# First weights from the standing pool, the residual in six parts, conditioning sums over both matrices, stores from ScalarE: edits to a seven-product MLP

## The chip, the cores and the metric

The kernel runs on one core of one Trainium2 chip. The core has a matrix engine (TensorE, PE in the profile) that multiplies operands in on-chip memory (SBUF) and accumulates into eight PSUM banks, and VectorE (DVE), ScalarE (ACT), GpSimd (POOL) and SyncE (SP), each with an instruction queue of its own that runs in order. Transfers between HBM and SBUF are started by an instruction on one of those queues and carried out by 16 DMA engines that all queues share. The metric is the device time of one execution in microseconds; less is better.

## What is computed

One step of a diffusion backbone with two layers on T = 1152 tokens (128 of context, 1024 latent), width 1024, all in fp32. Layer 0 mixes tokens with a recurrent block, layer 1 with latent attention. Behind each mixer stands a squared-ReLU MLP of hidden width 4096, and each sub-layer has an RMS norm, with shift, scale and gate from a linear map of the conditioning vector. The part that matters here, cut from the reference:

```python
def adaln_params(cond, w_ada, b_ada):
    mod = jax.nn.silu(cond) @ w_ada + b_ada
    return jnp.split(mod, 6, axis=-1)

def sq_relu_mlp(h, w1, w2):
    a = jax.nn.relu(h @ w1)
    return (a * a) @ w2
...
for l in range(DEPTH):
    sh1, sc1, g1, sh2, sc2, g2 = adaln_params(...)
    h = modulate(rms_norm(x, norm_mix[l]), sh1, sc1)
    out = mixer(h)
    x = x + g1[:, None, :] * out
    h = modulate(rms_norm(x, norm_mlp[l]), sh2, sc2)
    x = x + g2[:, None, :] * sq_relu_mlp(h, mlp_w1[l], mlp_w2[l])
y = rms_norm(x, final_norm)
```

Context and latent tokens have different conditioning vectors, so each row of `w_ada` is multiplied with two vectors.

## The kernel before

**Layout.** Activations are kept transposed (features on the 128 partitions, 8 blocks of 128 features), in three chunks of 384 tokens. Each fp32 matrix is split into a high and a low part. A product is then three matmuls (`mm3`, L146, L149, L150: high by high, high by low, low by high). The split is a cast on ScalarE (L164) and a subtraction (L165) on VectorE or GpSimd. A weight matrix of 128x1024 (512 KB, one row of `wts`) is loaded into a buffer `raw` (two of them in the standing pool `wp`), split into `whi` and `wlo`, and then `raw` is free.

**One MLP.** `mlp` runs once for each layer ("first" and "second MLP" below). Chunks 0 and 1 go through Winograd's form of Strassen's algorithm, seven block products in place of eight; chunk 2 is computed plainly beside them. The stages in program order:

1. *Fillers* (`filler`, L431): `filler(0, 8)`, eight plain 128-row blocks of the first matrix for chunk 2, 24 matmuls each, while the norms of chunks 0 and 1 are finished and `sums` (L390) makes the sums and differences of chunk 0 and 1 out of X. The norm itself is a generator (`norm_mod`, L294) that the filler steps move on: it yields a number of planned microseconds, `tick` (L359) counts them down.
2. *Up*: the pool of X is released and `upx` opened in its room. Sixteen steps `p`, each with weight sums on VectorE (L446) and seven products. Hidden results, after ReLU and square, are stored to HBM (`hid_d`, nine slots for each of eight groups, two row blocks of 192 KB to a slot) by `put` (L414), which issues on SP.
3. *Change-over*: `upx` is released, X gets new tiles in that room, and its three chunks (1.5 MB each, saved earlier to `xs_d`) are brought back by three DMAs. `load` (L547) brings `hid` tiles of 384 KB and splits them. `filler(8, 8)` does the other eight plain blocks.
4. *Down*: sixteen steps `d`, each with two rows of the second matrix and 22 sub-steps (`step`) of six matmuls; the last two steps leave chunk 2 out and have 14. A row of the second matrix gives two `whi`/`wlo` pairs, the plain one and the one of its differences, which GpSimd makes with four subtractions (L582). Results are added to X from PSUM as they come (`residual`, L332).
5. *End*: `after(0)` and `after(1)`, the next norm of chunks 0 and 1, are queued as generators behind `down2`, eight plain products for chunk 2. In the second MLP the norm is the last one, and its results are stored to the output.

The pairs `whi`/`wlo` take turns over slots as `wcycle` says: "wp" (three in the standing pool), "x" (one), "u" (one in `upx`), and in the down stage "c": a slot in the room of tiles with the tag "G", which also hold an operand of chunk 2 for the fillers.

**Conditioning.** The 56 jobs of `ada` (L175) each load 512 KB of `w_ada` into a `raw` buffer of `wp` and take two dot products on VectorE (L170, one for each conditioning vector). Eight are issued in layer 0's output projection, 40 in the up stage of the first MLP (two or three to a step `p`), and eight in its second set of fillers (`ada_rate`, one for each weight). None are left for the second MLP.

**What sets the order.** The program is not put on the queues in the order in which it is written. A planner simulates it with a time of its own for each instruction, and on each engine takes the ready instruction that stands first in the program. `keep_in_program_order` pins an instruction behind the one traced before it on its engine. A tile waits until the earlier user of its room has been read for the last time. All DMAs that the change touches are issued on SP.

Of the kernel before, what the change touches and what calls it, by code (L numbers as in the profile page):

```python
# [65 lines left out]
class Emit:  # L66
    def __init__(self, nc, tc, ins, outs):
        self.nc, self.tc, self.I, self.O = nc, tc, ins, outs
        self.piece_i = 0
        self.opened = []  # L70
        self.pending = []
        self.wpx = None
        self.pin = False
        self.cap = 1 << 30
        self.upx = None
        self.wcycle, self.wi = ["wp"], 0
        self.ready = []
        self.used, self.oldest = set(), 0
        self.ada_i = 0
        self.ada_jobs = []  # L80
        self.ada_quota = 0.0
        self.ada_rate = 0.0
# [31 lines left out]
    def wslot(self):  # L114

        kind = self.wcycle[self.wi % len(self.wcycle)]
        self.wi += 1
        if kind == "c":
            t = self.cbig(F32R, "wc", "G").rearrange("p a b -> p (a b)")
            return t[:, :1024], t[:, 1024:2048]  # L120
        pool, n = {"wp": (self.wp, 3), "x": (self.wpx, 1), "u": (self.upx, 1)}[kind]
        return tuple(pool.tile([128, 1024], F32R, tag=t, name=t, bufs=n) for t in ("whi", "wlo"))
# [51 lines left out]

    def ada(self, n):  # L175
        for l, j, k in self.ada_jobs[:n]:
            w = self.wp.tile([128, 1024], F32, tag="raw", name="raw", bufs=2)
            n0 = (j * 8 + k) * 128
            self.nc.sync.dma_start(w, self.I["ada_wt"][l, n0:n0 + 128])
            self.ada_dot(w, l, j, k, 0, 1)  # L180
            if k == 7:
                self.mod_finish(l, j)
        del self.ada_jobs[:n]
# [109 lines left out]

    def norm_mod(self, c, x, st, l, js, hi, lo, keep=False):  # L294
        nc = self.nc
        yield 4.0
        y = self.rstd(st, D)
        yield 5.0
        self.modulate(c, x, self.spread(y), l, js, hi, lo, keep=keep)
# [23 lines left out]
    def cbig(self, dt, name, tag="C"):  # L323
        return self.cpool.tile([128, 8, CH], dt, tag=tag, name=name, bufs=6 if tag == "C" else 3)

# [81 lines left out]
    def mlp(self, p0, base, l, H, after_acc, after):  # L407
# [5 lines left out]

        def put(m, slot, t):  # L414
            nc.sync.dma_start(hid_d[m // 4][:, slot, m % 2], t)

# [7 lines left out]
        def drain2(m, c, ps):  # L424
            t = self.cell(tag="acc")
            relu2(t, ps)
            put(m, 5, t)

        rhs = lambda k, c: (H[c][0][:, k], H[c][1][:, k])

        def filler(i0, n):  # L431
            for i in range(i0, i0 + n, 4):
                self.group([(plain[i + j], p0 + i + j, range(8)) for j in range(4)], rhs, drain2, chunks=[2])
# [15 lines left out]
        def prep(p, part):  # L449
            if p == 16:  # L450
                if part:
                    self.cap = p0 + 8 + part
                    self.prefetch(self.cap)
                return
            m = 4 * (p // 2) + p % 2
            if part == 0:
                r = [self.raw(up_row(i), self.upx, 4) for i in (m, m + 2)]
                W[p] = {"r": r, "R0": self.wsplit(r[0], leng)}
                return
            w = W[p]  # L460
            r0, r1 = w["r"]
            a, b = slice(0, 512), slice(512, 1024)
            if part == 1:
                w["R1"] = self.wsplit(r1[:, b], leng, 512)
                add(r0[:, a], r1[:, a], r0[:, a], ALU.subtract)
                add(r1[:, a], r1[:, b], r1[:, a], ALU.subtract)
                add(r1[:, b], r1[:, b], r0[:, a], ALU.subtract)
                add(r0[:, b], r0[:, b], r1[:, b], ALU.subtract)
            else:
                w["TY"] = self.wsplit(r1, nc.vector)  # L470
                w["TX"] = self.wsplit(r0, nc.vector)
# [5 lines left out]
        for p in range(16):  # L477
# [46 lines left out]
            def tail(m=m, A=A, w=w, h11=h11, h12=h12, h22=h22):  # L524
# [3 lines left out]
                add(s, h21, h22)  # L528
                put(m, 4, s)
                add(h21, h11, h21, ALU.subtract)  # L530
                put(m, 6, h21)
                add(d, s, h11, ALU.subtract)
                put(m, 3, d)
                e = st()
                add(e, h12, d, ALU.subtract)
                put(m, 7, e)

            self.ada(3 if p % 2 else 2)
        tail()
# [6 lines left out]

        def load(upto):  # L547
            while used[0] < min(upto, 72):
# [5 lines left out]
                hi, lo = t[:, o:o + 2], t[:, o + 2:o + 4]  # L554
                nc.sync.dma_start(lo.bitcast(F32), hid_d[i // 9][:, i % 9])
                self.split(hi, lo, lo.bitcast(F32))
                D[i] = (hi, lo)
                used[0] += 1

        load(4)  # L560
        for c in range(NCH):
            x = self.xp.tile([128, 8, CH], F32, tag="X", name="X")
            nc.sync.dma_start(x, self.xs_d[l][c])
            self.X.append(x)
        load(12)
        self.ada_rate = 1.0
        filler(8, 8)
        self.ada_rate = 0.0
        self.ada(len(self.ada_jobs))

        self.wcycle, self.wi = ["c", "wp", "wp", "wp", "x", "c", "c"], 0
        V = []
# [19 lines left out]
        prep_down(7)  # L592
        sts_done = []
        for d in range(16):
# [59 lines left out]
        self.wcycle, self.wi = ["wp", "wp", "wp", "x"], 0  # L654
        self.cap = 1 << 30
        self.later(0, after(0))
        self.later(1, after(1))

# [17 lines left out]
    def run(self, stop=99):  # L676
        nc, tc, I, O = self.nc, self.tc, self.I, self.O
        with (
# [21 lines left out]
            cp = self.alloc(name="cpool", bufs=1)  # L700
            self.cpool = cp
            self.ada_jobs = [(l, j, k) for l, j in ADA_ORDER for k in range(8)]
            self.first_half(stop)
# [252 lines left out]
    def rg_out(self, H, stop):  # L956
        nc, I, O = self.nc, self.I, self.O
        hs = self.hs
        nc.sync.dma_start(O["fin"], self.fin)
        self.release(*reversed(self.opened[1:]))  # L960
        self.wpx = self.alloc(name="wpx", bufs=1, side="right", reuse_waits="tile")
# [24 lines left out]
        def after(c):  # L986
            hi, lo = self.hpair2(c)
            nc.sync.dma_start(self.xmid[c], self.X[c])
            self.H3.append((hi, lo))
            yield from self.norm_mod(c, self.X[c], sts[c], 1, 0, hi, lo)  # L990

# [7 lines left out]
    def out_proj(self, pi, Z, l, j):  # L999
# [11 lines left out]
        def after(c):  # L1011
            hi, lo = H2[c] = self.hpair2((2, 0, 1).index(c))
            self.nc.sync.dma_start(self.xs_d[l][c], self.X[c])
            yield from self.norm_mod(c, self.X[c], sts[c], l, j + 1, hi, lo, keep=True)
            if c == 1:
# [25 lines left out]
    def mla(self):  # L1041
# [128 lines left out]
        self.need(None)  # L1170
        self.release(tab, self.cpool)
        self.attention(pi, ckv, kpe)
# [205 lines left out]
    def second_half(self):  # L1378
        nc, O = self.nc, self.O
        self.cpool = self.alloc(name="cpool2", bufs=1, reuse_waits="tile")  # L1380
        self.xp = self.alloc(name="xp2", bufs=3, side="right", reuse_waits="tile")
        Z, self.X = [], []
# [153 lines left out]
```

## Time and profile before

| what | us |
|---|---|
| runs of the kernel | 2876.41, 2880.87, 2880.27 |
| their median | 2880.27 |
| the profiled execution | 2878.42 |
| its span in the profile | 2876.7 |
| first MLP, from the first up product to the norm at its end | about 550 to 1350 |
| second MLP, to the end of the kernel | about 2120 to 2877 |

The page lists the busy time of each engine and, in forty slices of the span, its share. Below the page stand answers of the trace: groups of instructions by source line, the order of single instructions with what each waited for in brackets, and busy time in stretches of the span. In such a row, `ps<-hhi,whi` names what is written and what is read; `L146` is line 146 of the kernel; `[25.93 <-ACT whi L164]` says that the engine stood 25.93 us before this instruction, and that the ScalarE instruction of line 164, which wrote `whi`, released it. PEld is the loading of weights into TensorE. The granted clock is the share of full speed at which the chip ran TensorE.

The memory traffic is 126 GB/s over the span (268.83 MB read, 94.54 MB written).

### The profile page before, as it was taken

The page shows a single profiled execution, that of the slowest core. Times are in us where ns is not written, and L with a number is a line of the kernel's source. Part 1 is how long each engine was busy: PE and PEld are TensorE (multiplying, and loading weights), DVE is VectorE, ACT ScalarE, POOL GpSimd, SP SyncE. Part 2 cuts the span into 40 slices and gives each one's busy share as a digit, 9 for nine tenths or more (in the row PEclk, how much of TensorE's full clock was granted, in tenths as well). Part 3 has the DMA queues.
Part 4 walks back from the last instruction along what each step waited for, and adds up shares of the span by engine and source line. Part 5 has one row for each costly group of instructions (what it writes and reads, how often), then busy time and mean ns, then how long its engine had stood idle before and what let it go on. Part 6 is the DMA issues. An engine that isn't in the chain of part 4 may idle for free.

```text
span 2876.7 us, 41002 instructions
## 1 busy us (share of the span) xinstructions
PE 2655.0 (92%) x15355; PEld 2566.9 (89%) x15355; DVE 1920.1 (67%) x3445; ACT 1389.8 (48%) x2446; POOL 866.5 (30%) x560
## 2 busy tenths in 40 slices
PE   5999999699996899998997999998989999899997
PEld 2878899699995899997997999998989999899996
DVE  6788876999555577777364767762665555277777
ACT  3577834444453233234424878871455555233332
POOL 1000023121212777874242000001200001677773
PEclk9999999899998899999998999999999999999998
DMA  6122243577437334334135111116334445433342
GB/s 251 45 88 81 81 163 133 171 229 220 144 130 265 120 105 137 103 125 139 46 110 170 61 47 53 47 51 210 113 125 147 138 141 189 149 127 115 123 132 101
DMA packets 144855, 368.68 MB, mean 128 GB/s; under 512 B 15376, under 2 KB 77648, under 8 KB 141456
## 3 DMA queue, kind: packets, MB, share of 16 engines
q1 hardware_dynamic: 143888, 362.91, 37.9%
q0 software_dynamic: 768, 3.15, 0.4%
q8 instruction: 121, 1.98, 0.3%
q14 instruction: 78, 0.64, 0.1%
HBM read 268.83 MB, written 94.54 MB: 126 GB/s over the span
## 4 chain that ended last, share of the span: by engine, by line
PE 53%; DVE 5%; DMA 3%; POOL 3%; ACT 2%; issue 2%; SPq 0%; DVEq 0%; POOLq 0%; ACTq 0%
PE ps L146 14%; PE ps L149 13%; PE ps L150 13%; PE ps L1290 2%; DMA raw<-wts 1%; PE ps L1234 1%; PE ps L1237 1%; PE ps L1238 1%; PE ps L1236 1%; PE ps L1235 1%; PE ps L1316 1%; PE ps L1315 1%; POOL wlo L165 1%; PE ps L1314 1%; DMA hid<-hid 1%
## 5 line engine op out<-in xcount | busy, mean ns | idle before, releaser
L165 POOL TENSOR_TENSOR wlo<-raw,whi 128x1024 fp32r<-128x1024 f32 (+1 forms) x177 | 427.1, 2419 | 1643.6 <-ACT whi L164 1028.6
L146 PE MATMUL ps<-hhi,whi 128*128 128x384 f32 x1576 | 539.0, 345 | 76.8 <-ACT whi L164 63.6
L332 DVE SCALAR_TENSOR_TENSOR X<-ps,mod,X 128x384 f32<-128x384 f32 (+2 forms) x768 | 384.2, 536 | 304.7 <-PE ps L150 270.7
L149 PE MATMUL ps<-hlo,whi 128*128 128x384 f32 x1576 | 540.4, 343 | 13.0 <-DVE hlo L319 12.8
L164 ACT CAST whi<-raw 128x1024 fp32r<-128x1024 f32 (+1 forms) x293 | 290.9, 1001 | 539.8 <-PE ps L149 286.7
L150 PE MATMUL ps<-hhi,wlo 128*128 128x384 f32 x1576 | 535.7, 342 | 12.4 <-POOL wlo L165 12.1
L146 PEld LDWEIGHTS ps<-hhi,whi 128*128 128x128 f32 x1576 | 303.3, 193 | 89.1 <-ACT whi L164 67.4
L150 PEld LDWEIGHTS ps<-hhi,wlo 128*128 128x128 f32 x1576 | 303.2, 193 | 17.6 <-POOL wlo L165 16.1
L149 PEld LDWEIGHTS ps<-hlo,whi 128*128 128x128 f32 x1576 | 304.2, 193 | 15.7 <-DVE hlo L319 15.7
L146 PE MATMUL ps<-hid,whi 128*128 128x384 f32 x824 | 278.5, 340 | 8.6 <-ACT whi L164 4.7
L149 PE MATMUL ps<-hid,whi 128*128 128x384 f32 x824 | 278.1, 338 | 0.0
L150 PE MATMUL ps<-hid,wlo 128*128 128x384 f32 x824 | 272.7, 336 | 0.0
L582 POOL TENSOR_TENSOR raw<-raw 128x256 f32<-128x256 f32 x256 | 232.3, 917 | 13.8
L165 DVE TENSOR_TENSOR hid<-hid 128x768 fp32r<-128x768 f32 x144 | 203.8, 1425 | 46.0 <-ACT hid L164 45.8
L165 DVE TENSOR_TENSOR wlo<-raw,whi 128x1024 fp32r<-128x1024 f32 x116 | 134.2, 1167 | 137.6 <-ACT whi L164 137.0
L146 PE MATMUL ps<-hid,wc 128*128 128x384 f32 x584 | 195.6, 338 | 8.1 <-ACT wc L164 6.2
L149 PE MATMUL ps<-hid,wc 128*128 128x384 f32 x584 | 196.7, 337 | 0.0
L150 PE MATMUL ps<-hid,wc 128*128 128x384 f32 x584 | 193.5, 337 | 0.8 <-POOL wc L165 0.8
L164 ACT CAST hid<-hid 128x768 fp32r<-128x768 f32 x144 | 119.7, 836 | 135.7 <-DMA hid<-hid 109.4
L146 PEld LDWEIGHTS ps<-hid,whi 128*128 128x128 f32 x824 | 155.9, 189 | 12.8 <-ACT whi L164 6.6
L165 POOL TENSOR_TENSOR wc<-raw,wc 128x1024 fp32r<-128x1024 f32 x56 | 138.7, 2488 | 77.9 <-ACT wc L164 77.9
L1239 DVE TENSOR_REDUCE mx<-ps 128x1 f32<-128x384 f32 (+1 forms) x200 | 108.6, 543 | 79.7 <-PE ps L1238 78.1
(221 smaller groups left out, 6130.1 us busy)
## 6 DMA issues: line engine op xcount, KB each, us to landing
raw<-wts SPq DMA_DIRECT2D x221, 512.0 KB, 3.7
hid<-hid SPq DMA_DIRECT2D x144, 384.0 KB, 4.5
hid<-st SPq DMA_DIRECT2D x256, 192.0 KB, 1.9
raw<-ada_wt SPq DMA_DIRECT2D x56, 512.0 KB, 3.9
adaw<-ada_n SPq DMA_DIRECT2D x24, 512.0 KB, 4.4
xs<-X SPq DMA_DIRECT2D x6, 1536.0 KB, 5.4
X<-xs SPq DMA_DIRECT2D x6, 1536.0 KB, 10.1
o_d<-o SPq DMA_DIRECT2D x64, 128.0 KB, 1.7
```

Of the source, the lines that this page charges most:

```text
L146: mm = nc.tensor.matmul(ps, lhsT=w[0], rhs=h[0], start=first, stop=False, **kw)
L149: nc.tensor.matmul(ps, lhsT=w[0], rhs=h[1], start=False, stop=False, **kw)
L150: nc.tensor.matmul(ps, lhsT=w[1], rhs=h[0], start=False, stop=last, **kw)
L164: nc.scalar.copy(out=hi, in_=src)
L165: (lo_eng or nc.vector).tensor_tensor(out=lo, in0=src, in1=hi.bitcast(F32), op=ALU.subtract)
L332: self.nc.vector.scalar_tensor_tensor(out=self.X[c][:, m, a:b], in0=ps[:, a:b], scalar=self.mod[:, l, j, cond, m:m + 1], in1=self.X[c][:, ...
L582: sub = lambda out, x, y: nc.gpsimd.tensor_tensor(out=out, in0=x, in1=y, op=ALU.subtract)
L1234: nc.tensor.matmul(ps, lhsT=qh, rhs=kh[:, a:b], start=True, stop=False)
L1235: nc.tensor.matmul(ps, lhsT=qh, rhs=kl[:, a:b], start=False, stop=False)
L1236: nc.tensor.matmul(ps, lhsT=ql, rhs=kh[:, a:b], start=False, stop=False)
L1239: nc.vector.tensor_reduce(out=mx[:, j:j + 1], in_=ps, axis=AX.X, op=ALU.max)
L1290: nc.tensor.transpose(ps[:, j * 128:(j + 1) * 128], p[:, (t * 3 + j) * 128:(t * 3 + j + 1) * 128], self.ident)
```

## The change

1. The first pair of raw weights of the up stage (`p` = 0) is loaded into the two `raw` buffers of `wp` and no longer into `upx`.
2. X is brought back in six halves of 768 KB. Each is issued behind the drain of one filler of the second set (`bring`, called by `drain2`) and pinned there, and with it the next `hid` loads.
3. No conditioning jobs go with the fillers. The up stage takes 24 (one or two to a step), and the other 24 go to the down stage: each use of a slot "g" brings one. These slots are a new pool `gx` (four pairs and a tile `ada` for the conditioning rows), in the room of the former "G" tiles, which are now a pool of their own, `gpool`, released after the last filler. The order of slots in the down stage is four "g", three "wp", one "x".
4. `put` issues on ScalarE's queue, but for the four stores of `tail`, which stay on SP.
5. The store of X (to `xs_d`, and to `xmid` after the first MLP) is issued after the statistics of the norm, not before, and the second planned interval of the norm is 6.0 and not 5.0 us.
6. The norm of chunk 1 at the end of an MLP starts 10.0 planned microseconds later (`behind`).

```diff
@@ wslot
-        if kind == "c":
-            t = self.cbig(F32R, "wc", "G").rearrange("p a b -> p (a b)")
-            return t[:, :1024], t[:, 1024:2048]
-        pool, n = {"wp": (self.wp, 3), "x": (self.wpx, 1), "u": (self.upx, 1)}[kind]
+        if kind == "g":
+            self.ada(1, self.gx)
+        pool, n = {"wp": (self.wp, 3), "x": (self.wpx, 1), "u": (self.upx, 1), "g": (self.gx, 4)}[kind]
@@ ada
-    def ada(self, n):
+    def ada(self, n, room=None):
         for l, j, k in self.ada_jobs[:n]:
-            w = self.wp.tile([128, 1024], F32, tag="raw", name="raw", bufs=2)
+            w = (room or self.wp).tile([128, 1024], F32, tag="ada" if room else "raw", name="raw", bufs=1 if room else 2)
@@ norm_mod
         y = self.rstd(st, D)
-        yield 5.0
+        if store:
+            store()
+        yield 6.0
@@ mlp
-        def put(m, slot, t):
-            nc.sync.dma_start(hid_d[m // 4][:, slot, m % 2], t)
+        def put(m, slot, t, eng=nc.scalar):
+            eng.dma_start(hid_d[m // 4][:, slot, m % 2], t)
...
             put(m, 5, t)
+            if bring2:
+                bring2[0](plain.index(m) - 8)
...
-                r = [self.raw(up_row(i), self.upx, 4) for i in (m, m + 2)]
+                r = [self.raw(up_row(i), *((self.upx, 4) if p else ())) for i in (m, m + 2)]
...
-            self.ada(3 if p % 2 else 2)
+            self.ada(1 + p % 2)
...
-                nc.sync.dma_start(lo.bitcast(F32), hid_d[i // 9][:, i % 9])
+                ld = nc.sync.dma_start(lo.bitcast(F32), hid_d[i // 9][:, i % 9])
+                if pin:
+                    self.tc.keep_in_program_order(ld)
...
-        load(4)
         for c in range(NCH):
-            x = self.xp.tile([128, 8, CH], F32, tag="X", name="X")
-            nc.sync.dma_start(x, self.xs_d[l][c])
-            self.X.append(x)
+            self.X.append(self.xp.tile([128, 8, CH], F32, tag="X", name="X"))
+        xh = [(c, i) for c in range(NCH) for i in (0, 4)]
+
+        def bring(i):
+            if 2 <= i:
+                c, k = xh[i - 2]
+                self.tc.keep_in_program_order(
+                    nc.sync.dma_start(self.X[c][:, k:k + 4], self.xs_d[l][c, :, k:k + 4])
+                )
+            load((2, 4, 5, 6, 7, 8, 9, 9)[i], True)
+
+        filler(8, 8, bring)
         load(12)
-        self.ada_rate = 1.0
-        filler(8, 8)
-        self.ada_rate = 0.0
-        self.ada(len(self.ada_jobs))
-        self.wcycle, self.wi = ["c", "wp", "wp", "wp", "x", "c", "c"], 0
+        self.release(self.gpool)
+        self.gx = self.alloc(name="gx", bufs=1, reuse_waits="tile")
+        self.wcycle, self.wi = ["g", "g", "g", "g", "wp", "wp", "wp", "x"], 0
...
+        self.release(self.gx)
+        self.gpool = self.alloc(name="gpool3", bufs=1, reuse_waits="tile")
+        def behind(us, gen):
+            yield us
+            yield from gen
         self.later(0, after(0))
-        self.later(1, after(1))
+        self.later(1, behind(10.0, after(1)))
@@ after, in rg_out and in out_proj
-            nc.sync.dma_start(self.xmid[c], self.X[c])
...
+            ... store=lambda: nc.sync.dma_start(self.xmid[c], self.X[c])
```

More of the change, by code (lines that the diff above doesn't have):

```diff
@@ L74, in __init__ @@
         self.cap = 1 << 30
-        self.upx = None
+        self.upx = self.gx = None
         self.wcycle, self.wi = ["wp"], 0
@@ L292, in spread, with norm_mod @@
         return r
-    def norm_mod(self, c, x, st, l, js, hi, lo, keep=False):
+    def norm_mod(self, c, x, st, l, js, hi, lo, keep=False, store=None):
         nc = self.nc
@@ L323, in cbig @@
     def cbig(self, dt, name, tag="C"):
-        return self.cpool.tile([128, 8, CH], dt, tag=tag, name=name, bufs=6 if tag == "C" else 3)
+        pool, n = (self.cpool, 6) if tag == "C" else (self.gpool, 3)
+        return pool.tile([128, 8, CH], dt, tag=tag, name=name, bufs=n)
     def hpair2(self, i):
@@ L427, in drain2, with filler @@
             put(m, 5, t)
+            if bring2:
+                bring2[0](plain.index(m) - 8)
         rhs = lambda k, c: (H[c][0][:, k], H[c][1][:, k])
-        def filler(i0, n):
+        bring2 = []
+        def filler(i0, n, f=None):
+            if f:
+                bring2.append(f)
             for i in range(i0, i0 + n, 4):
@@ L528, in tail @@
                 add(s, h21, h22)
-                put(m, 4, s)
+                put(m, 4, s, nc.sync)
                 add(h21, h11, h21, ALU.subtract)
-                put(m, 6, h21)
+                put(m, 6, h21, nc.sync)
                 add(d, s, h11, ALU.subtract)
-                put(m, 3, d)
+                put(m, 3, d, nc.sync)
                 e = st()
                 add(e, h12, d, ALU.subtract)
-                put(m, 7, e)
-            self.ada(3 if p % 2 else 2)
+                put(m, 7, e, nc.sync)
+            self.ada(1 + p % 2)
         tail()
@@ L545, in mlp, with load @@
         used = [0]
-        def load(upto):
+        def load(upto, pin=False):
             while used[0] < min(upto, 72):
@@ L592, in mlp @@
         prep_down(7)
-        sts_done = []
         for d in range(16):
@@ L701, in run @@
             self.cpool = cp
+            self.gpool = self.alloc(name="gpool", bufs=1)
             self.ada_jobs = [(l, j, k) for l, j in ADA_ORDER for k in range(8)]
@@ L959, in rg_out @@
         nc.sync.dma_start(O["fin"], self.fin)
-        self.release(*reversed(self.opened[1:]))
+        self.release(*reversed(self.opened[2:]))
         self.wpx = self.alloc(name="wpx", bufs=1, side="right", reuse_waits="tile")
@@ L987, in after @@
             hi, lo = self.hpair2(c)
-            nc.sync.dma_start(self.xmid[c], self.X[c])
             self.H3.append((hi, lo))
-            yield from self.norm_mod(c, self.X[c], sts[c], 1, 0, hi, lo)
+            yield from self.norm_mod(
+                c, self.X[c], sts[c], 1, 0, hi, lo, store=lambda: nc.sync.dma_start(self.xmid[c], self.X[c])
+            )
         self.pi = self.mlp(pi, pi, 0, H2, lambda c, m: self.sq_acc(sts[c], self.X[c][:, m], m), after)
@@ L1012, in after @@
             hi, lo = H2[c] = self.hpair2((2, 0, 1).index(c))
-            self.nc.sync.dma_start(self.xs_d[l][c], self.X[c])
-            yield from self.norm_mod(c, self.X[c], sts[c], l, j + 1, hi, lo, keep=True)
+            yield from self.norm_mod(
+                c, self.X[c], sts[c], l, j + 1, hi, lo, keep=True,
+                store=lambda: self.nc.sync.dma_start(self.xs_d[l][c], self.X[c]),
+            )
             if c == 1:
@@ L1170, in mla @@
         self.need(None)
-        self.release(tab, self.cpool)
+        self.release(tab, self.gpool, self.cpool)
         self.attention(pi, ckv, kpe)
@@ L1380, in second_half @@
         self.cpool = self.alloc(name="cpool2", bufs=1, reuse_waits="tile")
+        self.gpool = self.alloc(name="gpool2", bufs=1, reuse_waits="tile")
         self.xp = self.alloc(name="xp2", bufs=3, side="right", reuse_waits="tile")
```

## The prediction, made before the changed kernel was run

> **What bounds the kernel now.** I read the page's table of engines first, then the busy time by stage, then the order of single instructions around each hole.
>
> ```profile
> PE 2655.0 (92%) x15355; PEld 2566.9 (89%) x15355; DVE 1920.1 (67%) x3445; ACT 1389.8 (48%) x2446; POOL 866.5 (30%) x560
> ```
>
> TensorE (PE) is busy for 92% of the span, so nearly everything is hidden behind it, and time can only come from where it stands still or runs slowly. The stages (window; length; then busy time and instruction count for PE, weight loads, VectorE, ScalarE, GpSimd; granted clock; DMA share; GB/s):
>
> ```profile
> 520.00:560.00 40.00, 13.90 (x65) 13.07 (x64) 36.15 (x43) 13.42 (x16) 6.39 (x3) 0.66 0.47 154
> 560.00:700.00 140.00, 131.23 (x725) 128.83 (x725) 138.06 (x207) 61.30 (x112) 28.11 (x13) 0.98 0.75 227
> 878.00:946.00 68.00, 36.41 (x146) 32.42 (x146) 31.62 (x52) 16.85 (x25) 14.49 (x7) 0.74 0.72 254
> 946.00:970.00 24.00, 20.36 (x94) 18.57 (x94) 7.00 (x13) 5.14 (x5) 20.30 (x18) 0.80 0.12 33
> 1000.00:1300.00 300.00, 296.94 (x1701) 295.28 (x1700) 224.96 (x344) 101.64 (x114) 230.21 (x158) 1.00 0.37 121
> 1300.00:1350.00 50.00, 36.09 (x206) 35.15 (x205) 44.77 (x90) 25.00 (x42) 23.49 (x13) 0.86 0.41 141
> 2100.00:2130.00 30.00, 16.69 (x82) 16.37 (x81) 24.24 (x24) 15.52 (x21) 0.00 (x0) 0.77 0.26 91
> 2130.00:2400.00 270.00, 270.00 (x1548) 270.00 (x1547) 143.28 (x212) 138.72 (x242) 0.00 (x0) 1.00 0.41 137
> 2430.00:2475.00 45.00, 34.09 (x168) 31.79 (x167) 7.45 (x10) 17.97 (x26) 19.47 (x11) 0.89 0.77 281
> 2475.00:2500.00 25.00, 23.13 (x123) 22.50 (x122) 9.68 (x20) 8.16 (x9) 21.49 (x17) 0.93 0.24 71
> 2820.00:2877.00 57.00, 36.50 (x209) 34.85 (x208) 42.17 (x99) 12.78 (x23) 16.02 (x11) 0.85 0.32 111
> ```
>
> In the window from 2130 nothing stalls: 1548 matmuls in 270 us, 0.1744 us each. With that price, a window's loss is its length less its count times 0.1744. First MLP: its start (520) loses 40 - 11.3 = 28.7 us; the next 140 us lose 13.6; the change from first to second matrix loses 42.5 (878) and 7.6 (946); the second matrix (1000) only 3.3; its end 14.1. Second MLP: start 15.7, change 15.7 and 3.5, end 20.5. These are the places that the diff touches. Part of each loss is a clock that is still low after a hole:
>
> ```profile
> 892.70 0.52 PE L150 MATMUL ps<-hhi,wlo 128*128 128x384 f32 x1
> 893.02 0.52 PE L146 MATMUL ps<-hhi,whi 128*128 128x384 f32 x1
> ```
>
> Here matmuls start 0.32 us apart (starts 892.70 and 893.02), not 0.174.
>
> **The change, part by part.** (a) *First weights in the standing pool.* The hole at each MLP's start, with what ran before it:
>
> ```profile
> 543.82 1.77 DVE L165 TENSOR_TENSOR S<-X,S 128x1536 fp32r<-128x1536 f32 x1
> 545.62 0.80 SPq L111 DMA_DIRECT2D raw<-wts  x2
> 550.56 0.69 PE L146 MATMUL ps<-hhi,whi 128*128 128x384 f32 x1 [25.93 <-ACT whi L164]
> 2121.09 0.69 PE L146 MATMUL ps<-hhi,whi 128*128 128x384 f32 x1 [13.31 <-ACT whi L164]
> ```
>
> The first raw weights live in `upx`, in the room of the residual X, so their load (545.62) waits for the last split of X (543.82 + 1.77); cast and TensorE follow. In `wp` they can be fetched while the eight fillers run. TensorE then has three products (12 matmuls x 0.1744 = 2.1 us each) that need no sum at all: R0 with A11, with A12 and half of P. What is late next is S2, behind VectorE:
>
> ```profile
> L170 DVE SCALAR_TENSOR_TENSOR junk<-raw,cb 128x1024 bf16<-128x1024 f32 x8 | 10.3, 1291 | 1.8 <-DMA raw<-ada_wt 1.8
> L170 DVE SCALAR_TENSOR_TENSOR raw<-raw,cb 128x1024 f32<-128x1024 f32 x8 | 9.8, 1227 | 0.0
> L398 DVE TENSOR_TENSOR X<-X 128x1536 f32<-128x1536 f32 x4 | 7.1, 1765 | 0.0
> ...
> L446 DVE TENSOR_TENSOR raw<-raw 128x512 f32<-128x512 f32 x128 | 91.7, 719 | 42.8 <-POOL wlo L165 41.8
> ```
>
> The first three rows are from 500 to 550 us, the last from the whole span. The conditioning dots take 20.1 us of VectorE beside the sums' 7.1. With both `raw` buffers of `wp` held by the first pair of weights, no conditioning load can start until that pair is split, and the dots leave the critical stretch; 4 x 0.7 us of weight sums and two splits (some 5 us) come in. I leave 7 of 28.7 us: **-22** (bounds -29 to -13). In the second MLP there are no dots to remove: 15.7 leaves 4: **-12** (-16 to -4). In the 140 us after the first start the up stage has 24 conditioning jobs instead of 40, but VectorE stays full (138.06 of 140) for as long as they are drained: **-2** (-8 to +2).
>
> (b) *The change-over.* Six fillers after 878 wait for one weight each:
>
> ```profile
> 902.92 0.33 SPq L179 DMA_DIRECT2D raw<-ada_wt  x1
> 905.14 0.33 SPq L111 DMA_DIRECT2D raw<-wts  x1
> 889.15 0.69 PE L146 MATMUL ps<-hhi,whi 128*128 128x384 f32 x1 [11.05 <-ACT whi L164]
> 945.62 0.69 PE L146 MATMUL ps<-hid,wc 128*128 128x384 f32 x1 [6.20 <-ACT wc L164]
> ```
>
> Weight and conditioning loads take turns in the two `raw` buffers (902.92, 905.14), so each weight is late. The conditioning leaves this stage. Each filler is 24 matmuls, 4.2 us, 33.5 us for eight. Two things stay. First, the `gx` slots lie in the room of chunk 2's operands, which the last filler still reads, so the first four matrices cannot be split ahead:
>
> ```profile
> L582 POOL TENSOR_TENSOR raw<-raw 128x256 f32<-128x256 f32 x128 | 116.2, 916 | 6.8
> L165 POOL TENSOR_TENSOR wlo<-raw,whi 128x1024 fp32r<-128x1024 f32 x37 | 92.3, 2505 | 36.5 <-ACT whi L164 25.5 <-PE ps L150 10.9
> L165 DVE TENSOR_TENSOR hid<-hid 128x768 fp32r<-128x768 f32 x60 | 90.0, 1508 | 15.2 <-ACT hid L164 15.2
> ```
>
> GpSimd needs 2 x 2.5 + 4 x 0.92 = 8.7 us for a pair, 17.4 for two, 18.5 with the first cast (about 1 us). Of the 22 steps of the first `d` (six matmuls, 1.05 us each) seven can run before the fourth matrix: 7.3 us, so 11 us of hole, and 3 more at the low clock: 14. Second, the loads:
>
> ```profile
> raw<-wts SPq DMA_DIRECT2D x221, 512.0 KB, 3.7
> hid<-hid SPq DMA_DIRECT2D x144, 384.0 KB, 4.5
> ...
> xs<-X SPq DMA_DIRECT2D x6, 1536.0 KB, 5.4
> X<-xs SPq DMA_DIRECT2D x6, 1536.0 KB, 10.1
> 880.00:890.00 10.00, 0.85 (x2) 0.50 (x2) 7.64 (x16) 4.34 (x6) 0.83 (x1) 0.53 1.05 418
> ```
>
> Eight weights, six halves of X, nine `hid` tiles (384 KB) and eight stores (192 KB) are 14.0 MB: 33.5 us at the 418 GB/s of this window, so no slack, and 55 us at the 254 of the whole 68. The halves, one behind each filler, keep the queue from holding weights behind 4.7 MB as now. I take 6 us for it. So 20 us stay where the first MLP loses 50.1: **-30** (-42 to -14), and where the second loses 19.2: **+1** (-11 to +11).
>
> (c) *Conditioning in the second matrix.* 24 jobs move there, 20 of them into the first ten `d` steps. A step is 132 matmuls, 23.0 us; VectorE is busy 224.96/300 of it, 17.3 us. Two jobs are four dots of about 1.26 us: 22.3, still under 23.0, so the low end is nothing. But VectorE is held up beside GpSimd:
>
> ```profile
> L165 DVE TENSOR_TENSOR hid<-hid x58: 944/1026/3169, 984.3 to 1278.4; 128x768 fp32r<-128x768 f32 x58
> ```
>
> The `hid` splits take 944 ns at least and 1508 on average: 0.56 us of waiting each. With that, four dots make 24.6: 1.6 us too much, 16 us in ten steps; below that, residual adds that free PSUM come late now and then. I take **+12** (0 to +36, the upper end below), nearest to the `hid` row, from the same stage.
>
> The Trainium skill (SBUF — State Buffer, "Who interferes with whom") speaks against this part: a VectorE instruction with two SBUF inputs and a GpSimd instruction that reads SBUF share a port, which one of them holds for its whole duration. The longest `hid` split above (3169) agrees with such a wait. As a mechanism of this kernel: GpSimd's 4 x 2.505 + 8 x 0.916, 4.5 `hid` splits at 0.944 and four dots at 1.26 are 26.6 us in a row, 3.6 over 23.0, +36 in ten steps.
>
> (d) *ScalarE issues stores.*
>
> ```profile
> 881.85 0.32 SPq L415 DMA_DIRECT2D hid<-acc  x1
> SPq L415 <- ACT st L418: 203.4, 104, 6.2
> ```
>
> SP takes 0.32 us for an issue and stood 203.4 us behind ScalarE's squares; that wait holds up loads queued behind it, but in the up stage from 2130 TensorE loses nothing by it. On ScalarE no issue is shown. With SP's price 80 per MLP are 26 us beside 138.72 of 270 busy; only some 32 issues lie where ScalarE is on the path (eight fillers at each start, eight at each change), 10 us at most. Below nothing: earlier loads, already counted in (b). I take **+2** (-3 to +10). The deferred stores of X keep their 5.4 us well ahead of the overwrite; one more step of planned delay (5.0 to 6.0 us) is inside the next term.
>
> (e) *Chunk 1's norm later.*
>
> ```profile
> 1341.24 0.87 PE L289 MATMUL ps<-ident,sy 128*128 128x128 f32 x3 [11.76 <-DVE sy L282]
> 2853.80 0.44 PE L289 MATMUL ps<-ident,sy 128*128 128x128 f32 x1 [6.65 <-DVE sy L282]
> ...
> L1410 DVE SCALAR_TENSOR_TENSOR X<-X,vec,ps 128x384 f32<-128x384 f32 x24 | 13.0, 609 | 2.1 <-PE ps L289 2.1
> ```
>
> TensorE stands before chunk 1's broadcast (L289), with matmuls that need it not queued behind. Ten us later, chunk 0's matmuls of the next layer go first: **-8** of 14.1 (-12 to -2), as chunk 0's own norm still has to run. At the end of the kernel the same hole closes, but chunk 1's eight scalings (4.3 us at the 13.0/24 of the last row) move to the tail: **-3** (-8 to +4).
>
> Sum: -22 -2 -30 +12 -8 -12 +1 -3 +2 = -62, from the profiled execution's 2878.4 (span 2876.7): 2816. The median of the runs is 1.9 above it: **2818 us**.
>
> **Rivals.** *The order is not what the edit says:* all orders come from the planner's own estimate, and it may still put conditioning loads ahead of the first weights. For: it did so at 902.92. Then (a)'s two starts stay: +34, 2852 us; 13%. *The change-over is bound by loads:* 55 instead of 33.5 us, 15.6 beyond the six counted, twice: 2849; for it the 254 and 281 GB/s rows, against it the 418; 12%. With the first one: 2883, no change; 3%. *The port of (c) is held throughout:* +24, 2842; 10%. *The holes close:* (a) leaves nothing (-11), (c) costs nothing (-12), the change-overs leave 10 each (-20): 2775; 7%. *Slower:* conditioning loads pace the second matrix as they paced the fillers. They have one tile, SP issues in order, so a load that waits for the last dot holds the weights and `hid` behind it. In (b) 42.5 us were lost beside eight such loads, 5.3 each: 24 x 5.3 = 127, 115 more than taken, 2933 us. It decides above (62 + 12)/24 = 3.1 us per load. Against it: eight split pairs stand ahead, two steps' worth, and weights no longer share the tile; 8%.
>
> **How the numbers follow.** The forecast has 47%, with its own range of 2795 to 2840. The range reaches to 2775 and 2860, taking in all but the slower cases, no change, and tails. About 0.2% (6 us) is what a measurement can tell: faster 0.89, within 0.03, slower 0.08.
>
> **What would show it.** (a) No wait over 8 us of TensorE before `whi` at either start, first raw loads issued during the fillers. (b) Fillers 4.2 us apart, and a hole of about 10 us before the first `wlo` of the second matrix. (c) VectorE over 90% busy there, dots at 1.6 to 1.9 us, TensorE waiting for X. (e) No 11.76 us before L289. I am wrong if the starts keep their holes, or if the second matrix of the first MLP loses over 36 us.

## The result and the profile after

| kernel | runs | median us | lowest to highest |
|---|---|---|---|
| before | 4 | 2879.39 | 2876.41 to 2880.87 |
| changed | 4 | 2859.96 | 2856.87 to 2862.01 |

The ratio is 0.9933 (95% interval 0.9916 to 0.995): 19 us faster, where 62 were forecast. The spans of the two profiled executions differ by 18.5 us (2876.7 and 2858.2).

The line of engines of the changed kernel, and then its busy time by stretches (window; length; busy time and count of PE, weight loads, VectorE, ScalarE, GpSimd; granted clock; DMA share; GB/s):

```profile
PE 2663.3 (93%) x15355; PEld 2566.0 (90%) x15355; DVE 1945.2 (68%) x3445; ACT 1384.3 (48%) x2446; POOL 893.0 (31%) x560
```

```profile
520.00:560.00 40.00, 35.58 (x189) 35.22 (x189) 36.66 (x42) 22.64 (x35) 6.67 (x4) 0.91 0.50 169
...
850.00:896.00 46.00, 32.95 (x165) 30.38 (x163) 15.33 (x21) 23.36 (x35) 14.26 (x6) 0.89 0.96 360
896.00:920.00 24.00, 16.99 (x66) 14.88 (x66) 19.94 (x24) 3.69 (x5) 22.06 (x14) 0.71 0.22 67
920.00:1140.00 220.00, 194.19 (x1042) 186.89 (x1043) 203.33 (x296) 63.28 (x70) 173.16 (x106) 0.96 0.48 158
1140.00:1300.00 160.00, 157.78 (x903) 156.24 (x902) 116.40 (x182) 53.75 (x63) 117.24 (x79) 1.00 0.35 112
...
2095.00:2130.00 35.00, 33.07 (x187) 32.19 (x187) 27.96 (x30) 21.61 (x31) 0.00 (x0) 1.00 0.50 177
...
2405.00:2447.00 42.00, 32.75 (x169) 30.98 (x169) 18.55 (x16) 22.57 (x34) 12.53 (x7) 0.92 0.93 357
```

At 0.1744 us for a matmul, the start of the first MLP now loses 40 - 33.0 = 7.0 us where it lost 28.7. The second matrix is the other way round: from 920 to 1140 it loses 220 - 181.7 = 38.3 us, with VectorE busy for 203 of 220. As soon as the conditioning is done (from 1140) it loses 2.5 in 160. The longest wait at the first start and the longest at the end of the first MLP are now these (idle time before the instruction, and its releaser, in brackets):

```profile
539.23 0.69 PE L148 MATMUL ps<-S,whi 128*128 128x384 f32 x1 [4.42 <-DVE S L164]
...
1326.13 0.69 PE L145 MATMUL ps<-hhi,whi 128*128 128x384 f32 x1 [4.96 <-ACT hhi L319]
```

The waits of 25.93 and 11.76 us are gone, and each has a shorter one in its place.

Both traces have 15355 matmuls. So they can be laid side by side by count: at which time has the same number been started? Negative is earlier than before.

| stage (time of the kernel before) | earlier or later at its end | change in the stage | forecast |
|---|---|---|---|
| up to the first MLP (520) | +1.5 | +1.5 | 0 |
| its start and up stage (840) | -24.6 | -26.1 | -24 |
| its change-over, to the first product of the second matrix (946) | -49.3 | -24.7 | -30 |
| second matrix, to the changed kernel's place at 1140 (1151) | -10.9 | +38.4 | +12 |
| second matrix, the rest (1300) | -8.5 | +2.4 | 0 |
| its end (1440) | -12.1 | -3.7 | -8 |
| second layer up to its MLP (2100) | -11.4 | +0.7 | 0 |
| start and up stage of the second MLP (2400) | -24.8 | -13.4 | -12 |
| its change-over, with the first products of the second matrix (2560) | -18.1 | +6.7 | +1 |
| its second matrix (2800) | -16.3 | +1.8 | 0 |
| end of the kernel | -18.5 | -2.2 | -3 |

The forecast's remaining +2, for the stores on ScalarE, has no stage of its own. Two places have gone wrong: the second matrix of the first MLP (26 us more than forecast), and the two change-overs (5 and 6 more). The -30 counts in a hole of 14 us behind the first product, where the kernel before lost 7.6. Counted where that hole lies, the first change-over is 12 us worse than forecast and the second matrix 20. The expectations below go by a coarser count, from windows of 10 us, which gave 37.7 for the 38.4.

What TensorE waited for in those 220 us of the changed kernel (in total, number of waits, longest):

```profile
PE ps L145 <- DVE X L334: 24.9, 18, 3.9
PE ps L145 <- ACT whi L163: 1.6, 1, 1.6
```

It waits for the residual adds (L334, L332 before the change), which free the PSUM banks. It is 26.5 us of standing. Most of the other 12 of the 38.3 are matmuls that start further apart after these holes, at a low clock (granted 0.96). VectorE's and GpSimd's groups from 920 to 1130:

```profile
L334 DVE SCALAR_TENSOR_TENSOR X<-ps,mod,X 128x384 f32<-128x384 f32 x103 | 59.5, 605 | 1.2 <-PE ps L149 1.0
L164 DVE TENSOR_TENSOR hid<-hid 128x768 fp32r<-128x768 f32 x30 | 49.7, 1666 | 1.1 <-ACT hid L163 1.1
L169 DVE SCALAR_TENSOR_TENSOR junk<-raw,cb 128x1024 bf16<-128x1024 f32 x21 | 39.6, 1885 | 12.4 <-DMA raw<-ada_wt 12.3
L169 DVE SCALAR_TENSOR_TENSOR raw<-raw,cb 128x1024 f32<-128x1024 f32 x21 | 33.8, 1610 | 0.1
...
L164 POOL TENSOR_TENSOR wlo<-raw,whi 128x1024 fp32r<-128x1024 f32 x33 | 88.7, 2698 | 41.0 <-ACT whi L163 40.0 <-issue 1.1
```

The dots take 1.885 and 1.610 us where I had 1.26 each without a stretch. VectorE also stands 12.3 us at the head of its queue before a conditioning load, with residual adds queued behind. One such pair of dots, on VectorE and on GpSimd, in order of time:

```profile
947.43 3.25 DVE L169 SCALAR_TENSOR_TENSOR junk<-raw,cb 128x1024 bf16<-128x1024 f32 x1
950.61 0.08 DVE L169 DVE_READ_ACCUMULATOR junk<-raw,cb 128x1 f32 x1
950.72 3.25 DVE L169 SCALAR_TENSOR_TENSOR raw<-raw,cb 128x1024 f32<-128x1024 f32 x1
953.90 0.08 DVE L169 DVE_READ_ACCUMULATOR raw<-raw,cb 128x1 f32 x1
953.90 3.48 DVE L334 SCALAR_TENSOR_TENSOR X<-ps,mod,X 128x384 f32<-128x384 f32 x8
```

```profile
947.19 5.69 POOL L164 TENSOR_TENSOR wlo<-raw,whi 128x1024 fp32r<-128x1024 f32 x2 [1.16 <-ACT whi L163]
952.96 2.40 POOL L599 TENSOR_TENSOR raw<-raw 128x256 f32<-128x256 f32 x2
```

Both dots last 3.25 us beside two splits on GpSimd; eight residual adds (953.90, x8) have piled up behind them.

### The profile page after: what moved, and what is told of

It reads as the page before. It is cut to its first block, busy times and chain, and to the rows that moved or that the text cites. A ratio compares the mean times of both kernels' runs of the same rounds, so it can differ in the third digit from the quotient of the medians.

```text
span 2858.2 us, 40872 instructions
## 1 busy us (share of the span) xinstructions
PE 2663.3 (93%) x15355; PEld 2566.0 (90%) x15355; DVE 1945.2 (68%) x3445; ACT 1384.3 (48%) x2446; POOL 893.0 (31%) x560
## 4 chain that ended last, share of the span: by engine, by line
PE 41%; DVE 5%; DMA 3%; POOL 2%; issue 2%; ACT 2%; SPq 0%; DVEq 0%; ACTq 0%; POOLq 0%
PE ps L145 9%; PE ps L148 9%; PE ps L149 9%; PE ps L1317 2%; DMA raw<-wts 2%; POOL wlo L164 1%; PE ps L1261 1%; PE ps L1264 1%; PE ps L1265 1%; PE ps L1262 1%; PE ps L1263 1%; PE ps L1343 1%; PE ps L1342 1%; PE ps L1341 1%; POOL raw L599 1%
## 5 line engine op out<-in xcount | busy, mean ns | idle before, releaser
L164 POOL TENSOR_TENSOR wlo<-raw,whi 128x1024 fp32r<-128x1024 f32 x233 | 569.8, 2453 | 1662.5 <-ACT whi L163 1399.2
L163 ACT CAST whi<-raw 128x1024 fp32r<-128x1024 f32 (+1 forms) x349 | 347.6, 1008 | 671.7 <-POOL raw L599 269.1
L145 PE MATMUL ps<-hhi,whi 128*128 128x384 f32 x1576 | 533.0, 342 | 22.0 <-ACT hhi L319 10.3
L148 PE MATMUL ps<-hlo,whi 128*128 128x384 f32 x1576 | 536.4, 340 | 13.7 <-DVE hlo L320 13.4
L145 PE MATMUL ps<-hid,whi 128*128 128x384 f32 x1408 | 480.0, 344 | 51.3 <-DVE X L334 33.5
L334 DVE SCALAR_TENSOR_TENSOR X<-ps,mod,X 128x384 f32<-128x384 f32 (+2 forms) x768 | 379.4, 534 | 204.8 <-PE ps L149 171.0
L148 PE MATMUL ps<-hid,whi 128*128 128x384 f32 x1408 | 477.8, 339 | 0.0
L149 PE MATMUL ps<-hid,wlo 128*128 128x384 f32 x1408 | 462.9, 339 | 2.5 <-POOL wlo L164 2.5
L145 PEld LDWEIGHTS ps<-hid,whi 128*128 128x128 f32 x1408 | 269.0, 191 | 67.1 <-DVE X L334 39.1
L149 PEld LDWEIGHTS ps<-hid,wlo 128*128 128x128 f32 x1408 | 267.1, 190 | 3.3 <-POOL wlo L164 3.3
L148 PEld LDWEIGHTS ps<-hid,whi 128*128 128x128 f32 x1408 | 269.8, 192 | 0.0
L599 POOL TENSOR_TENSOR raw<-raw 128x256 f32<-128x256 f32 x256 | 252.8, 990 | 17.9
L148 PE MATMUL ps<-S,whi 128*128 128x384 f32 x384 | 130.4, 340 | 6.1 <-DVE S L164 6.1
L149 PE MATMUL ps<-S,wlo 128*128 128x384 f32 x384 | 130.4, 340 | 1.6 <-DVE wlo L164 1.5
```

The costliest lines, as they stand in the source:

```text
L145: mm = nc.tensor.matmul(ps, lhsT=w[0], rhs=h[0], start=first, stop=False, **kw)
L148: nc.tensor.matmul(ps, lhsT=w[0], rhs=h[1], start=False, stop=False, **kw)
L149: nc.tensor.matmul(ps, lhsT=w[1], rhs=h[0], start=False, stop=last, **kw)
L163: nc.scalar.copy(out=hi, in_=src)
L164: (lo_eng or nc.vector).tensor_tensor(out=lo, in0=src, in1=hi.bitcast(F32), op=ALU.subtract)
L334: self.nc.vector.scalar_tensor_tensor(out=self.X[c][:, m, a:b], in0=ps[:, a:b], scalar=self.mod[:, l, j, cond, m:m + 1], in1=self.X[c][:, ...
```

## The experiments

Each kernel is the changed one with one edit, the last with two. Times are medians; ratios are to the kernel before, run beside it on the same chip (its medians there: 2880.25 for more jobs in the up stage, two tiles, one input and the unpinned spread; 2878.59 for all stores on SP, the norm, the first weights and the whole transfers of X; 2878.54 for all jobs in the up stage, the pinned spread, the fillers' stores and the last kernel). Stage losses are by count, as in the table above, against the changed kernel; "the second matrix" is that of the first MLP, from its first product (896.29 in the changed kernel) to the changed kernel's place at 1140. Up to 520 us, ahead of the stages that these edits touch, the profiles differ from the changed kernel's by -2.5 to +2.6 us, so a stage that moves by 2 or 3 us may be chance.

**More jobs in the up stage.**

```diff
-            self.ada(1 + p % 2)
+            self.ada(3 if p % 2 else 2)
```

> All 40 conditioning jobs of the first MLP go back to its up stage, none to its second matrix; all else as changed. Theory (the dots overfill VectorE in the second matrix, which lost 37.7 us there): these 37.7 go, and the up stage pays about 4 (it lost 13.6 us with 40 jobs and 9.4 with 24), so about 2826 us. Rival (the loss belongs to the new slots and the new order, not to the dots): over 2850.

Measured 2839.17 us, ratio 0.986 (0.9845 to 0.9874). The expectation had miscounted: 48 jobs are left after the output projection, so eight still went to the second matrix. Of its 38.4 us 26.0 went, the up stage paid 6.6, and the change-over 2.7. The 12.4 us that are left are 1.6 for each of the eight jobs.

**All jobs in the up stage.**

```diff
-            self.ada(1 + p % 2)
+            self.ada(3)
```

> All 48 jobs left after the output projection go to the up stage (three to a step; the kernel with two or three left eight for the second matrix). Theory (1.6 us for each job in the second matrix, 0.4 for each one more in the up stage): 37.7 less 3 go there, 9 come in above, about 2834. Rival (the first steps of the second matrix lose 12.7 us without any dots, for the slots that come free late): no better than the 2839 of the kernel with eight jobs there.

Measured 2834.92 us, ratio 0.9845 (0.9828 to 0.9861). In the second matrix all of the 38.4 us are gone (38.7); the up stage pays 11.3 and the change-over 1.8. TensorE's waits from 920 to 1140:

```profile
PE ps L145 <- DVE X L334: 2.6, 4, 1.2
PE ps L145 <- ACT whi L163: 0.8, 1, 0.8
```

So the jobs make the loss: 38.7/24 = 1.6 us for each there, as for each of the eight in the kernel above, and 11.3/24 = 0.5 in the up stage. The rival, that the new slots cost 12.7 us without dots, falls: nothing is left.

**Two tiles for the conditioning rows.**

```diff
-        pool, n = {..., "g": (self.gx, 4)}[kind]
+        pool, n = {..., "g": (self.gx, 3)}[kind]
...
-            w = (room or self.wp).tile([128, 1024], ..., bufs=1 if room else 2)
+            w = (room or self.wp).tile([128, 1024], ..., bufs=2)
...
-        self.wcycle, self.wi = ["g", "g", "g", "g", "wp", "wp", "wp", "x"], 0
+        self.wcycle, self.wi = ["g", "g", "g", "wp", "wp", "wp", "x"], 0
```

> Two tiles for conditioning rows in the second matrix in place of one, and three slots g in place of four (same room). Theory VectorE full: only its 12.3 us of waits for conditioning loads go, about 2848. Rival (dots that wait for their load at the head of VectorE's queue hold up the residual adds, and that is the whole loss): about 2825. If loads do not matter: 2860.

Measured 2851.99 us, ratio 0.9905 (0.9891 to 0.992). The first dot of each job from 890 to 1170, in this kernel, and then in the changed one:

```profile
L169 DVE SCALAR_TENSOR_TENSOR junk<-raw,cb 128x1024 bf16<-128x1024 f32 x24 | 49.4, 2060 | 2.3 <-DMA raw<-ada_wt 2.3
```

```profile
L169 DVE SCALAR_TENSOR_TENSOR junk<-raw,cb 128x1024 bf16<-128x1024 f32 x24 | 47.3, 1971 | 16.2 <-DMA raw<-ada_wt 16.1
```

The waits for loads went from 16.1 to 2.3 us, and the second matrix gained only 3.7; the dots became longer (2060 ns for 1971). So waiting for the loads is not the loss. Another 3.9 came from the second MLP's change-over and first products, which have no dots; that would be the slots, but it is little more than chance makes.

**Sums with one input.**

```diff
+            if room:
+                self.nc.vector.tensor_reduce(out=self.mod[:, l, j, cond, k:k + 1], in_=w, op=ALU.add, axis=AX.X)
+                continue
...
-            self.ada_dot(w, l, j, k, 0, 1)
+            self.ada_dot(w, l, j, k, 0, 1, room=room)
```

> The two dots of the jobs in the second matrix are replaced by sums over the same tile, which read one tile and not two (the products with the conditioning vectors are left out). Theory port (a VectorE instruction with two inputs in SBUF waits for GpSimd): the sums take about 1.2 us each where the dots took 1.75, VectorE has 23.5 us of work in a step of 23.0, and 20 to 30 of the 37.7 us go: about 2835. Rival (VectorE is merely full, nothing is held up): the sums take as long as the dots, 1.75, and it stays at 2860.

Measured 2827.64 us, ratio 0.9818 (0.9804 to 0.9833). The sums in this kernel (durations in ns, least, median, most; first and last start):

```profile
L170 DVE TENSOR_REDUCE mod<-raw x42: 1201/1208/1222, 920.2 to 1074.5; 128x1 f32<-128x1024 f32 x42
```

Not one of 42 sums is stretched, in the same stage, beside GpSimd's same work, while the dots had 1.2 to 3.4 us. The second matrix loses 32.9 us less, though the sums are still there and still wait for loads (7.3 us from 920 to 1140). A sum takes as long as a dot that nothing holds up (1.21), so what costs is the stretch.

**Spread over all steps.**

```diff
-            self.ada(1, self.gx)
+            self.gn = getattr(self, "gn", -1) + 1
+            if self.gn % 4 != 3:
+                self.ada(1, self.gx)
```

> The 24 jobs of the second matrix are spread over all of its steps, 1.5 to a step in place of 2. Theory of a threshold (27 us of VectorE for a step of 23.0; with 1.5 jobs it is 17.3 + 0.5 + 1.5 x 3.65 = 23.3 and fewer waits): most of the 37.7 us go, about 2832. Rival (each job costs 1.9 us whatever its density): 2860.

Measured 2859.68 us, ratio 0.9928 (0.9911 to 0.9944). It does not test the density: the planner takes a job as soon as the tile is free, and the dots still ended before 1150. So a second kernel pins the loads.

```diff
-        if kind == "g":
-            self.ada(1, self.gx)
...
-            self.nc.sync.dma_start(w, self.I["ada_wt"][l, n0:n0 + 128])
+            ld = self.nc.sync.dma_start(w, self.I["ada_wt"][l, n0:n0 + 128])
+            if room:
+                self.tc.keep_in_program_order(ld)
...
+            if d % 2 == 1:
+                self.ada(1, self.gx)
...
+            self.ada(1, self.gx)
             if d % 2 == 1:
                 load(9 * (g + 1) + 12)
```

> The 24 jobs of the second matrix, their loads pinned on SP behind the hid and weight loads of each step, so that one or two come to a step over all sixteen. (Spreading them in the program alone left them at 24 in the first 250 us.) Theory threshold (with 1.5 jobs VectorE has 22.8 to 23.3 us of work in a step of 23.0): most of the 37.7 us go, about 2835. Rival (1.6 us for each job, at any density: 8 jobs lost 12.7, 24 lost 37.7): 2860.

Measured 2857.53 us, ratio 0.9923 (0.9908 to 0.9938). The first dot of each job by window (window; length; VectorE's time and count for them, two instructions to a job; clock; DMA share; GB/s), in this kernel and then in the changed one; and all engines in 200 us of this kernel:

```profile
1000.00:1050.00 50.00, 4.73 (x6) 1.00 0.48 158
...
1200.00:1250.00 50.00, 4.73 (x6) 1.00 0.43 152
```

```profile
1000.00:1050.00 50.00, 9.65 (x10) 0.97 0.41 139
```

```profile
1000.00:1200.00 200.00, 184.90 (x1028) 180.56 (x1028) 172.53 (x259) 57.05 (x65) 155.45 (x95) 0.98 0.42 141
```

Now there are three jobs in 50 us, where the changed kernel has five, and VectorE is busy for 86%. It gains 23.0 us in the second matrix up to the place at 1140, but the jobs that are left take all but 1.7 of it back by the end of the MLP: the same 24 jobs at the same price. An engine that is too full would have been relieved. The price is by the job, at both densities and for eight jobs as for 24. One thing was not held fixed: from 920 to 1350 VectorE stands 33.5 us before conditioning loads here, against 16.1 in the changed kernel; the two tiles above show such waits to cost little, but not nothing.

**The stores.**

```diff
-        def put(m, slot, t, eng=nc.scalar):
+        def put(m, slot, t, eng=nc.sync):
```

> The hidden results' stores issue on SP again; all else as changed. Theory (ScalarE's issues are hidden, and SP's waits behind the squares held up nothing): within 3 us of 2860. Rival (SP's stores hold up the loads at the change from first to second matrix): 2865 to 2875.

Measured 2844.32 us, ratio 0.9883 (0.9865 to 0.9902): some 15 us, 6.3 of them in the first change-over, 7.8 in the second (both up to the first product of the second matrix), and under 1 in each up stage. The second kernel moves back only the fillers' stores:

```diff
-            put(m, 5, t)
+            put(m, 5, t, nc.sync)
```

> Only the stores of the fillers issue on SP, so that the halves of X, pinned behind them on SP, wait for each filler's drain; the stores of the up stage stay on ScalarE. Theory anchor (with the fillers' stores on ScalarE, nothing on SP holds the halves back, they run ahead of the fillers' weights, and that cost the 14 to 16 us which all stores on SP gave): about 2846. Rival (ScalarE loses by issuing stores): 2858 or more.

Measured 2847.83 us, ratio 0.9885 (0.987 to 0.99), not to be told from all stores on SP. SP's issues of weights, stores (`hid<-acc`) and X in the second change-over, first in the changed kernel, then in this one:

```profile
2416.12 0.33 SPq L111 DMA_DIRECT2D raw<-wts  x1
2416.51 0.47 SPq L579 DMA_DIRECT2D X<-xs  x1
...
2418.68 0.33 SPq L111 DMA_DIRECT2D raw<-wts  x1
2421.22 0.32 SPq L579 DMA_DIRECT2D X<-xs  x1
...
2422.05 0.43 SPq L579 DMA_DIRECT2D X<-xs  x1
...
2425.60 0.32 SPq L579 DMA_DIRECT2D X<-xs  x1
...
2427.85 0.32 SPq L579 DMA_DIRECT2D X<-xs  x1
...
2435.97 4.50 SPq L111 DMA_DIRECT2D raw<-wts  x2
```

```profile
2421.48 0.32 SPq L417 DMA_DIRECT2D hid<-acc  x1
2421.85 0.43 SPq L579 DMA_DIRECT2D X<-xs  x1
...
2424.89 0.33 SPq L111 DMA_DIRECT2D raw<-wts  x1
2425.32 0.38 SPq L417 DMA_DIRECT2D hid<-acc  x1
2425.75 0.48 SPq L579 DMA_DIRECT2D X<-xs  x1
...
2428.09 0.32 SPq L417 DMA_DIRECT2D hid<-acc  x1
```

A half of X is pinned behind the SP transfer traced before it. If that is the filler's store, the half waits for the filler. With the store on ScalarE nothing on SP waits for the filler, and four halves (2421.22 to 2427.85) run ahead of the next weight (2435.97). The first product of the second matrix starts at 2446.89 us there, and at 2437.15 in this kernel. Against the changed kernel this one gains 8.1 us in the second change-over and 4.0 in the first, up to that product.

**Whole transfers of X.** The branch of `bring` that fetches halves is left out, and ahead of the fillers stands:

```diff
+        for c in range(NCH):
+            nc.sync.dma_start(self.X[c], self.xs_d[l][c])
         filler(8, 8, bring)
```

> X is brought back by three whole transfers ahead of the second set of fillers, as before the change; all else as changed. Theory (whole transfers hold up the fillers' weights): 6 to 11 us more for each MLP, 2872 to 2882. Rival (the halves among the fillers compete with their weights just the same; the second MLP's change-over lost 6.9 us with them): 2850 to 2862.

Measured 2875.17 us, ratio 0.9986 (0.9976 to 0.9996): 8.2 us more by the place at 920, behind the first change-over, and 4.6 behind the second. Halves help even without their anchor.

**First weights in `upx` again.**

```diff
-                r = [self.raw(up_row(i), *((self.upx, 4) if p else ())) for i in (m, m + 2)]
+                r = [self.raw(up_row(i), self.upx, 4) for i in (m, m + 2)]
```

> The first raw weights are loaded into upx again, behind the last read of X; all else as changed. Theory (these loads made the two holes at the starts): 25.9 and 13.5 us come back, about 2899. Rival (the first start gained because the conditioning dots left it): only the second comes back, about 2874.

Measured 2888.67 us, ratio 1.0039 (1.0027 to 1.005). The longest waits at the two starts in this kernel:

```profile
550.62 0.69 PE L145 MATMUL ps<-hhi,whi 128*128 128x384 f32 x1 [25.65 <-ACT whi L163]
2121.88 0.69 PE L145 MATMUL ps<-hhi,whi 128*128 128x384 f32 x1 [13.37 <-ACT whi L163]
```

Both holes are back, although the up stage still has 16 jobs fewer than before the change. The first start costs 25 us by 580, of which the up stage gives 8 back by 700; the second costs 13.4. (The medians differ by 28.7 us, the profiles by 22.8: the profiled execution is the fastest of its seven.) But the dots have come back to the first start too. The first dot of each job from 500 to 550 us, in this kernel and then in the changed one:

```profile
L169 DVE SCALAR_TENSOR_TENSOR junk<-raw,cb 128x1024 bf16<-128x1024 f32 x8 | 10.7, 1333 | 1.4 <-DMA raw<-ada_wt 1.4
```

```profile
L169 DVE SCALAR_TENSOR_TENSOR junk<-raw,cb 128x1024 bf16<-128x1024 f32 x3 | 3.6, 1209 | 0.0
```

So at the first start this kernel does not tell the weights' place from the dots that it lets in. Five jobs more there are ten dots, some 12 us, which bounds the dots' share; the second start, which has no dots, is the place of the weights alone.

**Chunk 1's norm without the delay.**

```diff
-        self.later(1, behind(10.0, after(1)))
+        self.later(1, after(1))
```

> Chunk 1's norm at the end of each MLP is not put off by 10 planned us; all else as changed. Theory (the delay closed part of the hole before the broadcast): 4.6 us at the end of the first MLP and 3.2 at the end of the kernel come back, about 2868. Rival (they came from elsewhere): 2860.

Measured 2863.02 us, ratio 0.9946 (0.9931 to 0.9961). The broadcast's wait is back:

```profile
1331.57 0.87 PE L288 MATMUL ps<-ident,sy 128*128 128x128 f32 x3 [12.71 <-DVE sy L281]
```

The end of the first MLP takes 5.6 us more, and the next layer gives about 1 of it back. The end of the kernel takes 3.3 more, as expected: its broadcast waits longer here than in the changed kernel (second fence).

```profile
2836.26 0.90 PE L288 MATMUL ps<-ident,sy 128*128 128x128 f32 x3 [6.56 <-DVE sy L281]
```

```profile
2841.88 0.87 PE L288 MATMUL ps<-ident,sy 128*128 128x128 f32 x3 [4.38 <-DVE sy L281]
```

The totals are only 3 us apart, and the intervals of the two ratios overlap, so it is the stages that show it.

**All jobs in the up stage and all stores on SP.** The edits `self.ada(3)` and `eng=nc.sync` from above, together.

> All 48 jobs in the up stage, and all stores of hidden results on SP. Theory (the two losses are apart, and add up): 15 us below the kernel with the jobs alone, about 2819. Rival (the same room at the change-over is counted twice): less than 8 us below it.

Measured 2821.58 us (2821.22 to 2823.34), ratio 0.9798 (0.9783 to 0.9813): 13.3 below the jobs alone, so the two losses are apart and add up. It is faster than both kernels that were compared.

## Why the prediction was wrong

(a) Right, in place and size: -39.5 in both starts with their up stages, -36 forecast. S2 was indeed late next: the longest wait left at the first start is 4.42 us for a split of S, and the window loses the 7 us that were left for it. How that gain divides between the weights and the dots stays open: with the old place of the weights the hole and the dots come back together, and at most some 12 of the 25.65 us are the dots'.

(b) The step that failed reads "The halves, one behind each filler, keep the queue from holding weights behind 4.7 MB as now". It holds only as long as something on SP waits for the filler. Part (d) of the same change took that away. With the fillers' stores on SP the second change-over, with the first products behind it, comes out 2.7 us better than before (6.7 less 9.4), where +1 was forecast. In the first change-over the same edit brings 4.0 of the 12 us that are missing, and all stores on SP bring 6.3. The rest stays open; with the DMA engines busy for 0.96 of the time there (850 to 896), the rival that loads bound the change-over is not excluded for it.

(d) Costed at +2 with an upper end of +10; it measured about 15. I had counted what an issue takes on ScalarE and what it frees on SP. The up stages agree with that (under 1 us each). I had not asked what was pinned behind the store that left SP.

(c) Costed at +12, measured at +38.4 (38.7 by taking all the jobs away), just past the upper end of 36. The sign of being wrong was there too: from 920 to 1300 the changed kernel loses 38.3 + 2.5 = 40.8 us. The stretch was right: dots of 1.6 to 1.9 us were forecast, 1.61 and 1.885 came. The step from there was wrong. I compared VectorE's sum with the length of a step, 24.6 with 23.0, and priced only the overflow; residual adds that come late were "now and then". That step failed. The runs show the opposite: the loss follows the number of stretched dots and not the fill (1.4 jobs a step lose as much as 2.3, and a job costs 1.6 us with eight as with 24). TensorE's 24.9 us of waits for residual adds fit a stretched dot that stands ahead of adds which free a bank. That the 36 us of the upper end came near is luck: they were an overflow of 3.6 us a step, which is not the mechanism.

The rule of the Trainium skill (SBUF — State Buffer, "Who interferes with whom") that was weighed there agrees with these runs: dots with two SBUF inputs are held up beside GpSimd (1.885 and 1.610 us), sums with one are not (1.208).

(e) -3.7 and -2.2 for -8 and -3. At the end of the kernel it was right: without the delay 3.3 us come back. At the end of the first MLP it was mis-sized: the long wait went, but in its place stands the one of 4.96 us for the next layer's operand (L319).

Of the 43.5 us between forecast and result (62 less 18.5), (c) makes 26.4, the change-overs 11.0 (5.3 and 5.7), and (e) 5.1 (4.3 and 0.8); the rest are stages that moved by 1 to 3 us, no more than the profiles of the experiments differ up to 520 us. The measured time lies just inside the upper end of the stated range, 2860, but by two misses together, (c) and the change-overs, that no rival there had put together.

## What to carry to other kernels

Beside a busy GpSimd, price work on VectorE by its form and by what is queued behind it, not by whether it still fits: here a job of two 1.21 us dots cost 1.6 us of TensorE's time, at 86% fill too, and the same job as sums with one input 0.2. When a transfer moves to another queue, look for what was pinned or queued behind it: the store cost ScalarE nothing that shows, but on SP it had set the pace of the transfers behind it.

## What was not expected of the hardware

A VectorE dot that reads two tiles from SBUF takes 1.21 us when nothing holds it up, and 3.25 beside GpSimd in the pair shown above. GpSimd is slowed in turn. Its groups in the changed kernel among the dots (920 to 1130, first fence) and behind them (1150 to 1300), and then in the kernel with the sums (920 to 1130):

```profile
L599 POOL TENSOR_TENSOR raw<-raw 128x256 f32<-128x256 f32 x67 | 76.5, 1146 | 4.3
```

```profile
L164 POOL TENSOR_TENSOR wlo<-raw,whi 128x1024 fp32r<-128x1024 f32 x27 | 67.0, 2495 | 36.6 <-ACT whi L163 29.9 <-PE ps L149 6.6
L599 POOL TENSOR_TENSOR raw<-raw 128x256 f32<-128x256 f32 x48 | 44.1, 919 | 3.8
```

```profile
L164 POOL TENSOR_TENSOR wlo<-raw,whi 128x1024 fp32r<-128x1024 f32 x39 | 95.6, 2462 | 45.9 <-ACT whi L163 44.8 <-PE ps L149 1.2
L602 POOL TENSOR_TENSOR raw<-raw 128x256 f32<-128x256 f32 x73 | 65.1, 898 | 4.5
```

Among the dots a subtraction takes 1.146 us for 0.919, a split 2.698 for 2.495; among the sums neither is longer. A VectorE reduction of the same tile takes 1.201 to 1.222 us beside the same work, and residual adds, with one input in PSUM, 0.605. Whether it is the second read alone that makes the difference was not tried: the dot also writes a whole tile, though the residual add does so too.
